# One decoder layer on one Trainium2 core: nine of 22 K-tile pairs of the down projection as seven block products

## The chip, the cores and the metric

The kernel runs on one core of a Trainium2 chip. The metric is device microseconds of that core, the median of several runs. The engines have queues of their own that run in order: TensorE (PE, with weight loads shown as PEld), VectorE (DVE), ScalarE (ACT), GpSimd (POOL) and SyncE (SP, which here only issues DMAs).

## The reference

One layer of a hybrid decoder, 256 tokens, model width 2048, all in float32. What matters here is its last third:

```python
x = x + jnp.concatenate([ha, hb], axis=-1) @ w_out[i]          # mixers' output

h = rms_norm(x, ffn_norm_g[i])
u = h @ w_up[i]                                                # 2048 -> 2 * 5632
a, g = jnp.split(u, 2, axis=-1)
a = causal_dwconv(a, conv_w[i], conv_b[i])
x = x + (jax.nn.gelu(a, approximate=False) * g) @ w_down[i]    # 5632 -> 2048

gate = jax.nn.sigmoid(rms_norm(x, ple_norm_g[i]) @ w_ple_gate[i])
x = x + gate * (p[i].astype(x.dtype) @ w_ple_proj[i])
```

Before it stand the RMS norm, the combined input projection, four mLSTM heads and eight attention heads.

## The kernel before

Every matrix product is made of float32r parts: an operand is cast by ACT to `hi`, and DVE subtracts to get `lo = raw - hi`. A product of two operands is then three matmuls, hi·hi, hi·lo and lo·hi, accumulated in one PSUM bank. The activations lie transposed, 128 features on the partitions, as tiles of 512 columns: 256 tokens of `hi`, then 256 of `lo` (`hT`, `catT`, `x2T`, `uT`, `x3T`). The weights stream in from HBM.

`run_stream` (L208) drives everything. A block is 1024 weight elements per partition. For each block it issues the load from the SP queue (L221) three blocks ahead into one of three `raw` buffers, splits it (L236 cast on ACT, L238 subtraction on DVE) three blocks ahead into one of four `hi`/`lo` buffers, and calls the block's function, which issues the matmuls. A scheduler then orders each engine's queue; what it made is shown below.

The stages in order are: the input projection and the mixers (a pool `mix` that is closed at the end), the output projection (`token_group`, L247, `resid`, L693), the up projection (`wide_group`, L300), the down projection (`token_group` with `uT`, L781 to L783) and the gate stage (L806 to L808).

- The up projection makes 512 features at a time, eight blocks for `a` and eight for `g`. `up_a` (L732) and `up_g` (L754) read the four banks out, do the convolution and GELU on ACT and DVE, and write two K tiles of `uT` at a time (L765).
- The down projection goes over four groups of 512 output columns. A group has 22 blocks; a block is two K tiles of 128 features by 512 columns, so the 22 blocks are the 22 pairs of K tiles. A block is 2 token halves x 2 K tiles x 3 matmuls (L266, L267, L268) of 512 columns. At the end of each group `resid` adds the two banks to `xs` (L696), transposes four K tiles of `x3T` (L698, L154, with the split at L145 and L146) and sums squares (L160).
- The gate stage goes over five groups of columns: first one block of the p projection (banks of tag `aux`), then the blocks of the gate (`mm`), whose end (`gate_done`, L791) makes the sigmoid, multiplies, adds `xs` and stores.

PSUM has two rings of four banks, `mm` and `aux`. The transposed rows of p (`pT`) are made beside the mixers (`load_conv`, L113).

Of the kernel before, what the change touches and what calls it, by code (L numbers as in the profile page):

```python
# [32 lines left out]
BLK = 1024  # L33
RAW, PARTS = 3, 4
AHEAD_DMA, AHEAD_SPLIT = 3, 3
PAD = 48

# [5 lines left out]
def layer_kernel(  # L43
# [11 lines left out]
    bp = ctx.enter_context(tc.tile_pool(name="big", bufs=1))  # L55
    wp = ctx.enter_context(tc.tile_pool(name="w", bufs=3))
    ps = ctx.enter_context(tc.tile_pool(name="ps", bufs=4, space=bass.MemoryType.PSUM))

# [3 lines left out]
    def f32(ap):  # L62
        return ap.bitcast(F32)
# [3 lines left out]

    g1 = cp.tile([16, P], F32, name="g1")
    act.dma_start(out=g1, in_=mix_norm_g[0].rearrange("(k c) -> k c", c=P))
# [18 lines left out]
    pool.memset(neghalf, -0.5)  # L88
    vrows = cp.tile([42, P], F32, name="vrows")
    for lo, n, src in (  # L90
# [19 lines left out]
    cT = cp.tile([P, 4 * KF], F32, name="cT")  # L110
    pT = bp.tile([P, 2, 512], F32R, name="pT")

    def load_conv(mp):  # L113
        def gen():
            cs = mp.tile([P, 512], F32, tag="qk", name="cs", bufs=2)
            act.dma_start(out=cs[0:88, 0:128], in_=conv_w[0, 0:2].rearrange("w (k c) -> (w k) c", c=P))
            act.dma_start(out=cs[0:44, 128:256], in_=conv_w[0, 2].rearrange("(k c) -> k c", c=P))
            act.dma_start(out=cs[44:88, 128:256], in_=conv_b[0].rearrange("(k c) -> k c", c=P))
            pr = mp.tile([P, 512], F32, tag="qk", name="pr", bufs=2)
            act.dma_start(out=pr.rearrange("p (t d) -> p t d", t=NT), in_=p[0, 0].rearrange("(t p) d -> p t d", p=P))  # L120
# [6 lines left out]
            yield  # L127
            bk = bank("aux", "pTp")
            for k in range(2):
                for t in range(NT):  # L130
                    pe.transpose(bk[:, k * 256 + t * P : k * 256 + (t + 1) * P],
                                 pr[:, t * 256 + k * P : t * 256 + (k + 1) * P], ident)
            for k in range(2):
                split_T(pT[:, k, :], bk[:, k * 256 : (k + 1) * 256])
            yield
        side.append(gen())
# [185 lines left out]

    apool = ctx.enter_context(tc.tile_pool(name="acts", bufs=1))
    aT = {}

    def new_aT(name):
        aT["cur"] = apool.tile([P, KD, 512], F32R, tag="aT", name=name)
        return aT["cur"]
# [3 lines left out]

    with tc.tile_pool(name="mix", bufs=1) as mp:
        catT = mp.tile([P, KD, 512], F32R, name="catT")

# [13 lines left out]

        hT = new_aT("hT")  # L350
        ssq1 = sm.tile([P, NT, 8], F32, name="ssq1")
        r1 = {}
# [367 lines left out]

    with tc.tile_pool(name="ffn", bufs=1) as fp:
        uT = fp.tile([P, KF, 512], F32R, name="uT")
# [3 lines left out]
        gl = {}  # L726

        def merge(dst, b):
# [3 lines left out]
        def up_a(q):  # L732
            st = {}

            def f(jj, b):
                pair, j = divmod(jj, 2)
                if j == 0:
                    st["a"] = fp.tile([P, 2, S], F32, tag="a", name="a", bufs=2)
                    st["c"] = gl[q, pair] = fp.tile([P, 2, S], F32, tag="gl", name="c", bufs=3)
# [12 lines left out]
            return f  # L752

        def up_g(q):  # L754
            st = {}

            def f(jj, b):
                pair, j = divmod(jj, 2)
                if j == 0:
                    st["u"] = fp.tile([P, 2, S], F32, tag="a", name="u", bufs=2)  # L760
                u, k = st["u"], 4 * q + 2 * pair
                merge(u[:, j], b)
                if j == 1:
                    dve.tensor_mul(u, u, gl.pop((q, pair)))
                    split_T(uT[:, k : k + 2, :], u)  # L765
            return f

        blocks = []
        x2 = aT["cur"]
        for q in range(KF // 4):  # L770
            blocks.extend(wide_group(w_up, q * 512, lambda: x2, up_a(q), "mm"))
            blocks.extend(wide_group(w_up, FF + q * 512, lambda: x2, up_g(q), "aux"))
        ssq3 = sm.tile([P, NT, 4], F32, name="ssq3")
# [17 lines left out]
        def gate_done(c0, n, last):  # L791
# [12 lines left out]
            return f  # L804

        for c0, n in ((0, 512), (512, 512), (1024, 512), (1536, 256), (1792, 256)):  # L806
            blocks.extend(token_group(w_ple_proj, [0], lambda: pT, c0, n, proj_done, tag="aux"))
            blocks.extend(token_group(w_ple_gate, all_k, get_x3T, c0, n, gate_done(c0, n, c0 == 1792)))  # L808
        run_stream(blocks, 0)

# [29 lines left out]
```

## Time and profile before

| | |
|---|---|
| median of 3 runs | 1286.85 us (1286.49 to 1286.88) |
| profiled execution, device time | 1286.34 us |
| its span | 1284.6 us |
| granted TensorE clock | 1.00 |
| moved by DMA | 238.69 MB, mean 186 GB/s |

The profile shows one execution. "Busy" of an engine is the time in which an instruction of it runs, and matmuls overlap each other, so a busy PE says only that it is not waiting. The table by stretches gives, for a window of the span, the busy time of each engine with the number of its instructions, the granted clock, the busy share of the DMA engines and GB/s. In the timeline, the bracket behind a row is the idle time of the engine ahead of it and what ended it.

### The profile page before, as it was taken

Reading aid. Unit: us, or ns where it says so; the run is one execution under the profiler, and the core shown is the slowest. Engines: PE = TensorE matmul, PEld = TensorE weight load, DVE = VectorE, ACT = ScalarE, POOL = GpSimd, SP = SyncE. Lnnn points to the kernel's source line nnn. Section 1 sums busy time; section 2 is a strip of 40 time slices with the busy share of each in tenths; the row PEclk is TensorE's granted clock in tenths of the full one; section 3 lists DMA queues with packets and bytes.
Section 4 is the critical chain, followed back from the end, with each engine's and each line's share of the span. In section 5 each row is a group of like instructions: output and inputs, shape, how many; then the busy total and the mean of one; then the engine's idle time right before and its main releaser. Section 6 shows DMA issues by size and latency. Waiting matters only on the chain.

```text
span 1284.6 us, 18150 instructions
## 1 busy us (share of the span) xinstructions
PE 1278.1 (99%) x7060; PEld 1123.1 (87%) x7060; DVE 754.3 (59%) x1008; ACT 650.7 (51%) x964; POOL 18.0 (1%) x33
## 2 busy tenths in 40 slices
PE   9999999999999999999999999999999999999998
PEld 7899999988888888888888888888888888888888
DVE  5455566554565565766676576767654545445554
ACT  7655454445554464655555455545543434444443
POOL 2000000000000000000000000000000000000000
PEclk9999999999999999999999999999999999999999
DMA  8676854556565666666666666666656566656663
GB/s 258 170 188 185 220 158 139 161 147 173 175 186 183 186 180 196 186 191 188 191 195 184 194 188 191 183 196 195 186 191 196 187 193 189 194 189 192 202 204 124
DMA packets 132040, 238.69 MB, mean 186 GB/s; under 512 B 7946, under 2 KB 28018, under 8 KB 131954
## 3 DMA queue, kind: packets, MB, share of 16 engines
q1 hardware_dynamic: 131072, 237.07, 62.8%
q8 instruction: 55, 0.90, 0.3%
q10 hardware_dynamic: 657, 0.43, 0.1%
q14 instruction: 32, 0.25, 0.1%
q0 software_dynamic: 224, 0.03, 0.0%
HBM read 235.40 MB, written 2.10 MB: 185 GB/s over the span
## 4 chain that ended last, share of the span: by engine, by line
PE 98%; DMA 1%; DVE 0%; ACT 0%; issue 0%; SPq 0%; DVEq 0%
PE wg L316 25%; PE tg L267 17%; PE tg L268 17%; PE tg L266 17%; PE wg L317 13%; PE fg L292 2%; PE fg L294 2%; PE fg L293 2%; DMA raw<-in_w_in_dram 1%; PE xT L154 1%; PE mob L609 0%; PE msc L583 0%; PE qkp L507 0%; PE sc L523 0%; PE ob L548 0%; PE rowb L494 0%
## 5 line engine op out<-in xcount | busy, mean ns | idle before, releaser
L238 DVE TENSOR_TENSOR lo<-raw,hi 128x1024 fp32r<-128x1024 f32 (+2 forms) x462 | 546.4, 1184 | 474.0 <-ACT hi L236 472.0
L236 ACT CAST hi<-raw 128x1024 fp32r<-128x1024 f32 (+2 forms) x462 | 470.6, 1019 | 557.3 <-PE tg L268 271.2
L316 PE MATMUL wg<-x2T,hi 128*128 128x512 f32 x1408 | 488.3, 392 | 0.0
L317 PE MATMUL wg<-x2T,lo 128*128 128x256 f32 x1408 | 393.5, 280 | 0.0
L316 PEld LDWEIGHTS wg<-x2T,hi 128*128 128x128 f32 x1408 | 264.1, 188 | 56.4
L317 PEld LDWEIGHTS wg<-x2T,lo 128*128 128x128 f32 x1408 | 267.3, 190 | 0.1
L266 PE MATMUL tg<-hi,uT 128*128 128x512 f32 x352 | 137.2, 390 | 0.0
L267 PE MATMUL tg<-lo,hT 128*128 128x512 f32 (+1 forms) x384 | 136.6, 356 | 0.5 <-DVE lo L238 0.5
L267 PE MATMUL tg<-lo,uT 128*128 128x512 f32 x352 | 137.0, 389 | 0.0
L268 PE MATMUL tg<-hi,uT 128*128 128x512 f32 x352 | 137.0, 389 | 0.0
L266 PE MATMUL tg<-hi,hT 128*128 128x512 f32 (+1 forms) x384 | 136.0, 358 | 0.0
L268 PE MATMUL tg<-hi,hT 128*128 128x512 f32 (+1 forms) x384 | 135.6, 354 | 0.0
L267 PEld LDWEIGHTS tg<-lo,hT 128*128 128x128 f32 x384 | 72.2, 188 | 8.1 <-DVE lo L238 0.9
L268 PEld LDWEIGHTS tg<-hi,hT 128*128 128x128 f32 x384 | 72.1, 188 | 7.4
L268 PEld LDWEIGHTS tg<-hi,uT 128*128 128x128 f32 x352 | 66.1, 188 | 13.7
L266 PEld LDWEIGHTS tg<-hi,uT 128*128 128x128 f32 x352 | 66.1, 188 | 13.7
L267 PEld LDWEIGHTS tg<-lo,uT 128*128 128x128 f32 x352 | 66.1, 188 | 13.6
L266 PEld LDWEIGHTS tg<-hi,hT 128*128 128x128 f32 x384 | 71.8, 188 | 6.9
L292 PE MATMUL fg<-hT,hi 128*128 128x256 f32 x256 | 74.3, 290 | 0.0
L294 PE MATMUL fg<-hT,lo 128*128 128x256 f32 x256 | 72.8, 284 | 0.0
L293 PE MATMUL fg<-hT,hi 128*128 128x256 f32 x256 | 72.4, 283 | 0.0
L267 PE MATMUL tg<-lo,x3T 128*128 128x512 f32 (+1 forms) x160 | 55.5, 347 | 0.0
(212 smaller groups left out, 1183.7 us busy)
## 6 DMA issues: line engine op xcount, KB each, us to landing
raw<-in_w_up_dram SPq DMA_DIRECT2D x176, 512.0 KB, 3.9
raw<-in_w_down_dram SPq DMA_DIRECT2D x88, 512.0 KB, 4.8
raw<-in_w_in_dram SPq DMA_DIRECT2D x79, 512.0 KB, 3.8
raw<-in_w_in_dram SPq DMA_DIRECT2D x48, 344.0 KB, 3.4
raw<-in_w_out_dram SPq DMA_DIRECT2D x32, 512.0 KB, 4.0
raw<-in_w_ple_gate_dram SPq DMA_DIRECT2D x32, 512.0 KB, 4.6
xs<-in_x_dram SPq DMA_DIRECT2D x8, 256.0 KB, 6.5
raw<-in_w_ple_proj_dram SPq DMA_DIRECT2D x3, 512.0 KB, 4.5
```

The costliest lines, as they stand in the source:

```text
L154: pe.transpose(bk[:, t * P : (t + 1) * P], xs[:, t, k * P : (k + 1) * P], ident)
L236: act.copy(hi, raw[:, :w])
L238: dve.tensor_sub(lo, raw[:, :w], f32(hi))
L266: pe.matmul(o, ah, hi[:, i, :], start=first, stop=False)
L267: pe.matmul(o, ah, lo[:, i, :], start=False, stop=False)
L268: pe.matmul(o, al, hi[:, i, :], start=False, stop=last)
L292: pe.matmul(o, hi[:, i, cols], a[:, 0:256], start=first, stop=False)
L293: pe.matmul(o, hi[:, i, cols], a[:, 256:512], start=False, stop=False)
L294: pe.matmul(o, lo[:, i, cols], a[:, 0:256], start=False, stop=last)
L316: pe.matmul(o, hi[:, i, cols], a, start=first, stop=False)
L317: pe.matmul(o[:, 256:512], lo[:, i, cols], a[:, 0:256], start=False, stop=last)
```

## The change

The down projection goes over two groups of 1024 columns instead of four of 512. In a group, a plain pair of K tiles is two units, each one K tile by 1024 columns, with eight block products in all (2 K tiles x 2 token halves x 2 column halves). Nine of the 22 pairs (2, 4, ... 18) take seven block products by the Strassen scheme in Winograd's form, in four units. The left operand's four sums (tokens x K) are made in the up stage by `left_sums`, split, written to HBM from POOL's queue, and read back once for each group from SP's. The right operand's four sums are made by DVE in place in the two raw buffers. Eight banks are open in a group: four output blocks, of which (1, 1) is fed by plain pairs alone, and four for the products P1, P5, P6, P7. After the ninth such pair `sums_done` adds the four to `xs`; after the last pair `add_rest` adds the others.

For this the raw buffers grow from three to five and the split buffers from four to seven in that part (they use the two temporaries of the up stage and the space of `x2T`), the activations get two buffers in one pool (`uT` becomes `uA` and `uB`), p is loaded and transposed at the start of the down projection, and the p projection of each gate group stands in the middle of its gate blocks. `run_units` takes the place of `run_stream` from the up projection on.

```diff
+RAW2, PARTS2 = 2, 3
+SEVEN = (2, 4, 6, 8, 10, 12, 14, 16, 18)
...
+        def left_sums(p_, u):
+            (a11, a21), (a12, a22) = ((u[:, j, 0:P], u[:, j, P:S]) for j in range(2))
+            f = sm.tile([P, 512], F32, tag="junk", name="Sf").rearrange("p (i c) -> p i c", i=4)
+            dve.tensor_add(f[:, 0], a21, a22)
+            dve.tensor_sub(f[:, 1], f[:, 0], a11)
+            dve.tensor_sub(f[:, 2], a11, a21)
+            dve.tensor_sub(f[:, 3], a12, f[:, 1])
+            t = fp.tile([P, 4, 256], F32R, tag="pT", name="Sp")
+            act.copy(t[:, :, 0:P], f)
+            dve.tensor_sub(t[:, :, P:256], f, f32(t[:, :, 0:P]))
+            pool.dma_start(out=sums[SEVEN.index(p_)], in_=f32(t).rearrange("p i c -> p (i c)"))
...
+        def run_units(us, first_late):
...
+                while True:
+                    if loaded < len(us) and held + len(us[loaded].srcs) <= RAW + RAW2 * more:
+                        us[loaded].load(loaded)
...
+                    elif split < min(loaded, i + PARTS + PARTS2 * more):
+                        us[split].split(split)
...
+                u.fn(*u.parts)
...
+            def product(key, ah, al, hi, lo):
...
+                pe.matmul(o, ah, hi, start=first, stop=False)
+                pe.matmul(o, ah, lo, start=False, stop=False)
+                pe.matmul(o, al, hi, start=False, stop=last)
...
+                def split1(hi, lo):
+                    v = late["S"][:, SEVEN.index(p_) % 2]
+                    nc.sync.dma_start(out=f32(v).rearrange("p i c -> p (i c)"), in_=sums[SEVEN.index(p_)])
+                    st["S"] = v
+                    part(hi[:, 0:512], lo[:, 0:512], first.raws[0][:, 0:512])
+                def fn1(hi, lo):
+                    product("P1", *left(k, 0), half(hi, 0), half(lo, 0))
+                def split2(hi, lo):
+                    part(hi, lo, first.raws[1])
+                def fn2(hi, lo):
+                    product((0, 0), *left(k + 1, 0), half(hi, 0), half(lo, 0))
+                    product((0, 1), *S(4), half(hi, 1), half(lo, 1))
+                def split3(hi, lo):
+                    ra, rb_ = first.raws
+                    dve.tensor_sub(half(ra, 0), half(ra, 1), half(ra, 0))
+                    dve.tensor_sub(half(ra, 1), half(rb_, 1), half(ra, 1))
+                    part(hi, lo, ra)
+                def fn3(hi, lo):
+                    product("P5", *S(1), half(hi, 0), half(lo, 0))
+                    product("P7", *S(3), half(hi, 1), half(lo, 1))
+                def split4(hi, lo):
+                    ra, rb_ = first.raws
+                    dve.tensor_sub(half(rb_, 1), half(rb_, 1), half(ra, 0))
+                    dve.tensor_sub(half(rb_, 0), half(rb_, 0), half(rb_, 1))
+                    part(hi, lo, rb_)
+                def fn4(hi, lo):
+                    product((1, 0), *left(k + 1, 1), half(hi, 0), half(lo, 0))
+                    product("P6", *S(2), half(hi, 1), half(lo, 1))
...
-        for c in range(4):
-            blocks.extend(token_group(w_down, list(range(0, KF, 2)), lambda: uT, c * 512, 512,
-                                      resid(c, ssq3, get_x3T, g_ple)))
...
+        us += down(0, "mm", "aux", sums_done(0), add_rest(0), {0: make_pT})
+        us += down(1024, "aux", "mm", sums_done(1024), add_rest(1024),
+                   {40: transposes(0), 41: transposes(2), 42: transposes(4, 6)})
```

Here `part(hi, lo, raw)` is the cast and the subtraction of before, the second and third arguments of `down` are the rings of the output banks and of the P banks, and `transposes(k)` makes two K tiles of `x3T`.

How the queues stand, at three places. Names carry running numbers; `hi248` is the `hi` part of unit 248, and `w2` is the space of `x2T`, which holds three of the seven split buffers and the left sums. On PE, one block of the down projection before, two K tiles by 512 columns:

```order
L266 MATMUL tg0_10185<-hi261_10471,uT_4383 128x512
L267 MATMUL tg0_10185<-lo261_10472,uT_4383 128x512
L268 MATMUL tg0_10185<-hi261_10471,uT_4383 128x512
L266 MATMUL tg0_10185<-hi261_10471,uT_4383 128x512
L267 MATMUL tg0_10185<-lo261_10472,uT_4383 128x512
L268 MATMUL tg0_10185<-hi261_10471,uT_4383 128x512
```

On PE after the change, the first four of the seven products of pair 4 in the second group (`dn(t, n)` are the output banks):

```order
L882 MATMUL dnP1_9950<-hi248_9945,uA_4373 128x512
L883 MATMUL dnP1_9950<-lo248_9946,uA_4373 128x512
L884 MATMUL dnP1_9950<-hi248_9945,uA_4373 128x512
L882 MATMUL dn(0, 0)_9875<-w2_8987,uA_4373 128x512
L883 MATMUL dn(0, 0)_9875<-w2_8987,uA_4373 128x512
L884 MATMUL dn(0, 0)_9875<-w2_8987,uA_4373 128x512
L882 MATMUL dn(0, 1)_9879<-w2_8987 128x512
L883 MATMUL dn(0, 1)_9879<-w2_8987 128x512
L884 MATMUL dn(0, 1)_9879<-w2_8987 128x512
L882 MATMUL dnP5_9970<-w2_8987 128x512
L883 MATMUL dnP5_9970<-w2_8987 128x512
L884 MATMUL dnP5_9970<-w2_8987 128x512
```

A product keeps its three matmuls of 512 columns; P7, (1, 0) and P6 follow. On DVE, inside the down projection before, nothing stands between the `lo` subtractions:

```order
L238 TENSOR_TENSOR lo236_9994<-raw236_9991,hi236_9993 128x1024
L238 TENSOR_TENSOR lo237_10012<-raw237_10009,hi237_10011 128x1024
L238 TENSOR_TENSOR lo238_10030<-raw238_10027,hi238_10029 128x1024
L238 TENSOR_TENSOR lo239_10048<-raw239_10045,hi239_10047 128x1024
L238 TENSOR_TENSOR lo240_10066<-raw240_10063,hi240_10065 128x1024
```

On DVE after, pair 6 of the first group (units 192 to 195) with the plain pair behind it (units 196, 197):

```order
L837 TENSOR_TENSOR lo192_9170<-raw192_0_9108,hi192_9169 128x512
L837 TENSOR_TENSOR w2_8987<-raw192_1_9110,w2_8987 128x1024
L930 TENSOR_TENSOR raw192_0_9108<-raw192_0_9108 128x512
L931 TENSOR_TENSOR raw192_0_9108<-raw192_1_9110,raw192_0_9108 128x512
L940 TENSOR_TENSOR raw192_1_9110<-raw192_1_9110,raw192_0_9108 128x512
L837 TENSOR_TENSOR lo196_9212<-raw196_0_9126,hi196_9211 128x1024
L941 TENSOR_TENSOR raw192_1_9110<-raw192_1_9110 128x512
L837 TENSOR_TENSOR w2_8987<-raw192_0_9108,w2_8987 128x1024
L837 TENSOR_TENSOR lo197_9230<-raw197_0_9139,hi197_9229 128x1024
L837 TENSOR_TENSOR w2_8987<-raw192_1_9110,w2_8987 128x1024
```

Where four `lo` subtractions stood for two pairs, there are six, of them one half as wide, and four half-wide subtractions in place. SP's queue issues the loads for the next pair of seven products in this order (the sum comes from `sums`):

```order
L822 DMA raw198_0_9189<-in_w_down_dram 128x1024
L913 DMA w2_8987<-sums_4390 128x1024
L822 DMA raw202_0_9203<-in_w_down_dram 128x1024
L822 DMA raw198_1_9191<-in_w_down_dram 128x1024
L822 DMA raw203_0_9215<-in_w_down_dram 128x1024
```

The two halves of a pair are now two loads, with others between. The third place is the start of the gate stage. On PE before, the gate's first matmuls follow the last of the down projection:

```order
L267 MATMUL tg1_10186<-lo263_10508,uT_4383 128x512
L268 MATMUL tg1_10186<-hi263_10507,uT_4383 128x512
L266 MATMUL tg0_10629<-hi265_10543,x3T_9306 128x512
L266 MATMUL tg1_10630<-hi265_10543,x3T_9306 128x512
L267 MATMUL tg0_10629<-lo265_10544,x3T_9306 128x512
```

On PE after:

```order
L884 MATMUL dn(1, 1)_9887<-w2_8987,uB_4374 128x512
L149 MATMUL xT0_10667<-ident_94,xs_81 128x128 x2
L149 MATMUL xT1_10672<-ident_94,xs_81 128x128 x2
L149 MATMUL xT2_10695<-ident_94,xs_81 128x128 x2
L261 MATMUL tg0_10775<-w2_8987,x3T_10666 128x512
L262 MATMUL tg0_10775<-w2_8987,x3T_10666 128x512
```

On ACT after, at the same place:

```order
L836 CAST w2_8987<-raw305_0_10616 128x1024
L155 ACTIVATE junk_10761,ssq3_4391<-xs_81 128x512
L836 CAST w2_8987<-raw306_0_10634 128x1024
L140 ACTIVATE x3T_10666<-xT0_10667,vT_113 128x256
L140 ACTIVATE x3T_10666<-xT1_10672,vT_113 128x256
```

The sixteen K tiles of `x3T` now all stand behind the last matmul of the down projection, and the first of their casts stands behind the cast of unit 306.

More of the change, by code (lines that the diff above doesn't have):

```diff
@@ L88, in layer_kernel @@
     pool.memset(neghalf, -0.5)
-    vrows = cp.tile([42, P], F32, name="vrows")
+    vrows = mp.tile([42, P], F32, name="vrows")
     for lo, n, src in (
@@ L126, in gen @@
             dve.tensor_copy(cT, bk[:, :176])
[L127 to L134, printed above, removed]
             yield
@@ L350, in layer_kernel @@
         hT = new_aT("hT")
+        catT = new_aT("catT")
         ssq1 = sm.tile([P, NT, 8], F32, name="ssq1")
@@ L726, in layer_kernel, with temp @@
         gl = {}
+        sums = kp.tile([len(SEVEN), P, 1024], F32, name="sums")
+        def temp(name):
+            return fp.tile([P, BLK], F32, tag="tmp", name=name, bufs=RAW2)
         def merge(dst, b):
@@ L764, in f @@
                     dve.tensor_mul(u, u, gl.pop((q, pair)))
-                    split_T(uT[:, k : k + 2, :], u)
-            return f
[L768 to L772, printed above, removed]
+                    dst = uA[:, k : k + 2, :] if k < KD else uB[:, k - KD : k - KD + 2, :]
+                    split_T(dst, u)
@@ new lines, in layer_kernel, with __init__, load, split @@
+        class Unit:
+            def __init__(self, srcs, fn, split=None, frees=1, shift=0):
+                self.srcs, self.fn, self.own, self.frees, self.shift = srcs, fn, split, frees, shift
+            def load(self, j):
+                self.raws = []
+                for i, src in enumerate(self.srcs):
+                    kb, n = src.shape[1], src.shape[2]
+                    raw = new_raw(f"raw{j}_{i}")
+                    nc.sync.dma_start(out=raw[:, : kb * n].rearrange("p (k n) -> p k n", k=kb), in_=src)
+                    self.raws.append(raw)
+            def split(self, j):
+                hi, lo = new_parts(j, self.shift)
+                if self.own is not None:
+                    self.own(hi, lo)
+                    self.parts = hi, lo
+                    return
+                kb, n = self.srcs[0].shape[1:3]
+                part(hi[:, : kb * n], lo[:, : kb * n], self.raws[0][:, : kb * n])
+                self.parts = [v[:, : kb * n].rearrange("p (k n) -> p k n", k=kb) for v in (hi, lo)]
@@ new lines, in part, with units @@
+        def part(hi, lo, raw):
+            act.copy(hi, raw)
+            dve.tensor_sub(lo, raw, f32(hi))
+        def units(blocks):
+            return [Unit([b[0]], b[1], shift=b[4] if len(b) > 4 else 0) for b in blocks]
+        def run_units(us, first_late):
+            loaded = split = held = 0
+            for i, u in enumerate(us):
+                if i == first_late:
+                    w2 = new_aT("w2").rearrange("p k n -> p (k n)")
+                    v = w2[:, 0 : 6 * BLK].rearrange("p (u n) -> p u n", n=BLK)
+                    late.update(hi=v[:, 0:3], lo=v[:, 3:6], S=w2[:, 6 * BLK :].rearrange("p (b i c) -> p b i c", b=2, c=256))
+                more = i >= first_late
+                while True:
+                    if loaded < len(us) and held + len(us[loaded].srcs) <= RAW + RAW2 * more:
+                        us[loaded].load(loaded)
+                        held += len(us[loaded].srcs)
+                        loaded += 1
+                    elif split < min(loaded, i + PARTS + PARTS2 * more):
+                        us[split].split(split)
+                        held -= us[split].frees
+                        split += 1
+                    else:
+                        break
+                u.fn(*u.parts)
```

154 lines of the change are left out of this document (138 added, 16 removed).

## The prediction

> **What bounds the kernel now.** I read the page's busy table and chain first, then the table by stretches, then the timeline of single instructions.
>
> ```profile
> PE 1278.1 (99%) x7060; PEld 1123.1 (87%) x7060; DVE 754.3 (59%) x1008; ACT 650.7 (51%) x964; POOL 18.0 (1%) x33
> PE 98%; DMA 1%; DVE 0%; ACT 0%; issue 0%; SPq 0%; DVEq 0%
> ```
>
> PE is busy for 1278.1 of 1284.6 us, and the chain that ended last runs on PE for 98% of the span. The time is the number of matmuls times their spacing, plus 6.5 us at both ends.
>
> ```profile
> 460.00:937.70 477.70, 477.70 (x2759) 422.43 (x2758) 322.78 (x453) 257.23 (x346) 0.00 (x0) 1.00 0.66 190
> 937.70:1180.00 242.30, 242.30 (x1083) 200.88 (x1082) 120.13 (x115) 102.65 (x116) 0.00 (x0) 1.00 0.61 191
> 1180.00:1280.00 100.00, 100.00 (x547) 87.30 (x546) 52.73 (x60) 43.94 (x52) 0.69 (x1) 1.00 0.58 183
> ```
>
> The three stretches are the up projection, the down projection and the gate stage (columns: length, then busy PE, PEld, DVE, ACT, POOL, granted clock, DMA share, GB/s). PE has no gap in any of them and its granted clock is 1.00. In the down stretch DVE is busy 120.13 of 242.30 us, ACT 102.65, DMA engines 0.61 at 191 GB/s: that is the room which the change draws on.
>
> The instructions that read `uT` (count, least/median/greatest ns, first and last start), and three matmuls of the timeline (start, length):
>
> ```profile
> L266 PE MATMUL tg<-hi,uT x352: 389/389/476, 937.9 to 1179.3; 128*128 128x512 f32 x176
> ```
>
> ```profile
> 957.68 0.39 PE L266 MATMUL tg<-hi,uT 128*128 128x512 f32 x1
> 957.91 0.39 PE L267 MATMUL tg<-lo,uT 128*128 128x512 f32 x1
> 958.13 0.39 PE L268 MATMUL tg<-hi,uT 128*128 128x512 f32 x1
> 958.36 0.39 PE L266 MATMUL tg<-hi,uT 128*128 128x512 f32 x1
> ```
>
> One matmul's 0.39 us overlaps the next. What counts is the spacing: 958.36 − 957.68 = 0.68 us for three, **0.2267 us** each. 352 x 3 = 1056 of them give 239.4 of the 242.3 us; the rest is transposes.
>
> **The change, part by part.** *Matmuls removed.* A seven-product pair issues 21 instead of 24 matmuls for 1024 columns, of the same 128x512 shape. Nine pairs in two column groups: 9 x 2 x 3 = 54 fewer, and the order of the new program has 1002 where 1056 stood. With PE never waiting, 54 x 0.2267 = **−12.24 us**.
>
> The Trainium skill, "TensorE: Matmul & The Clock Gate", section "Back-to-back issue gap", gives an isolated warm matmul N/2.4 + 2.5 ns, 215.8 ns for 512 columns; by that the term would be an estimated 11.65 us. The row's spacing is 226.7 ns, so the row decides.
>
> *Work added to VectorE and ScalarE.* Two pieces of the timeline, of DVE and of ACT:
>
> ```profile
> 938.46 0.68 DVE L764 TENSOR_TENSOR u<-u,c 128x512 f32<-128x512 f32 x1
> 939.10 1.23 DVE L238 TENSOR_TENSOR lo<-raw,hi 128x1024 fp32r<-128x1024 f32 x1
> 940.24 0.42 DVE L730 TENSOR_TENSOR u<-wg,u 128x256 f32<-128x256 f32 x1
> 940.58 0.68 DVE L143 TENSOR_TENSOR uT<-u,uT 128x512 fp32r<-128x512 f32 x1
> 941.18 0.68 DVE L764 TENSOR_TENSOR u<-u,c 128x512 f32<-128x512 f32 x1
> ```
>
> ```profile
> 913.05 1.05 ACT L236 CAST hi<-raw 128x1024 fp32r<-128x1024 f32 x1 [1.72 <-PE wg L316]
> 914.01 0.37 ACT L729 COPY a<-wg 128x256 f32<-128x256 f32 x1
> ```
>
> Back to back, a 1024-wide two-input op holds DVE for 940.24 − 939.10 = 1.14 us and a 512-wide one for 941.18 − 940.58 = 0.60 us; a cast holds ACT for 0.96 us. The in-place subtraction of half a weight tile has no row of its own; L764 reads two SBUF tiles of that size, so I take 0.60 us (0.68 if nothing overlaps). A seven-product pair needs four of these, one 512-wide and three 1024-wide `lo`: 5 x 0.60 + 3 x 1.14 = 6.42 us (7.12 with no overlap). A plain pair needs 2 x 1.14 = 2.28 us. They alternate, so a period of both is 8.70 us of DVE (9.57 by durations) against 45 x 0.2267 = **10.20 us of PE**. ACT has 0.56 + 5 x 0.96 = 5.4 us. PE keeps the longer total; the queue order decides whether it waits. The printed orders hide each cast behind another subtraction (`lo196` and `lo197` stand between the dependent ones), so I charge no steady loss, 0 to +9 us.
>
> *Weight buffers.* A seven-product pair holds two of the five raw buffers until its third and fourth splits. The page's DMA issues (count, KB, median us to landing), the landings of all raw loads, and the first 30 us by engine:
>
> ```profile
> raw<-in_w_down_dram SPq DMA_DIRECT2D x88, 512.0 KB, 4.8
> ```
>
> ```profile
> DMA to landing us min/median/max: 2.8/4.0/6.9
> ```
>
> ```profile
> 0.00:30.00 30.00, 27.74 (x136) 23.13 (x137) 17.99 (x28) 23.00 (x55) 7.17 (x23) 1.00 0.87 261
> ```
>
> In the looser order shown (pair of `raw192`) the first half is free 6.42 us after the pair begins on DVE. The next pair's second half is loaded into that buffer (the queue has `raw198_1` last), lands 4.8 us later and is wanted 1.2 us into that pair: a loop of 6.42 + 4.8 − 1.2 = 10.0 us, 0.2 us under PE's 10.2. In the tighter order it is 8.9. From a landing of about 5.0 us the looser loop is the longer. The demand is five 0.524 MB loads (four weights, one stored sum) in 10.2 us, 257 GB/s; the first 30 us moved 261 GB/s at a share of 0.87, so it fits. Working the first three seven-product pairs through by these durations, DVE waits about 1.9 us for each second half and is level with PE at `hi195`/`lo195`; afterwards it pulls ahead. I charge **+0.7 us**, ends 0 and +6.
>
> The Trainium skill, "DMA: Bandwidth & Descriptors", section "Anatomy of one DMA", fits 2.0 us plus bytes/436 GB/s for POOL-issued transfers, an estimated 3.2 us here; by it the loop would be 8.4 us and this term zero. The median landing in the trace is 4.8 us, so I keep the row.
>
> *Left sums.* Nine times in the up stage: four 128-wide subtractions, a 512-wide cast and `lo`, one 512 KB write from POOL's queue.
>
> ```profile
> 34.20 0.28 DVE L167 TENSOR_SCALAR dg<-ident,rstd_mix 128x128 f32<-128x128 f32 x1
> ```
>
> No two-input 128-wide row exists; 0.28 us has one input, 0.42 us twice the width; I take 0.28. 9 x (4 x 0.28 + 0.68) = 16 us raise DVE from 322.8 to 339 of 477.7 us. Four units of split weights (2.7 us of PE each) cover a burst of 1.8 us: cost 0; without cover at most 16 us. POOL has 0.00 us of work in that stretch, and the first sum is read back long after it is written.
>
> *Moved work.* The input-p transposes and casts move from the mixer to the first down unit: the same instructions, 0. The group sums and residual additions are about 5.2 + 2.4 us of DVE per half, beside three and two plain pairs: 0. The end of the second half is different. Its four result banks are the `aux` ring that the x3T transposes need, so now **all** of them stand behind the last matmul; before, 12 of 16 were done.
>
> ```profile
> 1179.77 0.39 PE L268 MATMUL tg<-hi,uT 128*128 128x512 f32 x1
> ...
> 1180.20 1.06 ACT L236 CAST hi<-raw 128x1024 fp32r<-128x1024 f32 x1 [1.67 <-PE tg L268]
> ...
> 1184.77 1.03 PE L154 MATMUL xT<-ident,xs 128*128 128x128 f32 x8
> 1185.40 1.57 ACT L145 ACTIVATE x3T<-xT,vT 128x256 fp32r<-128x256 f32 x4 [1.43 <-PE xT L154]
> 1185.56 0.48 PE L266 MATMUL tg<-hi,x3T 128*128 128x512 f32 x1
> 1185.91 1.66 DVE L146 SCALAR_TENSOR_TENSOR x3T<-xT,vT,x3T 128x256 fp32r<-128x256 f32 x4 [0.68 <-ACT x3T L145]
> ```
>
> On ACT the cast of `raw306` stands ahead of the first x3T cast, and its target is freed by the last down matmul: it starts 0.2 us after that matmul's slot (1180.20 against 1179.77 + 0.23) and holds ACT 0.96 us. The x3T cast takes about 0.48 more, so the first gate matmul comes near 1.7 us. PE has 0.3 us of transposes meanwhile (eight take 0.8 us): 1.4 us idle. The fifth transpose pair then waits about 0.45 us for a bank, which DVE reads only after `lo306`. Sum **+1.8 us**; queued behind that cast are all x3T casts, for which PE waits. Ends: 0 (the cast lands early) and +4.
>
> Sum: −12.24 + 0.7 + 1.8 = −9.7. The profiled execution is 1286.34 us, its span of 1284.6 plus 1.74 around it, giving 1276.6. The median of the runs lies 0.5 above it: **1277.1 us**.
>
> **The rivals.**
>
> *DVE is the bound in the seven-product periods.* In-order waits push its 9.57 us of durations past 10.2, say to 10.7. For: PE is in order too, and a late `lo` holds every product behind it. Against: room of 0.6 to 1.5 us. 18 x 0.5 = 9 us, less some 2 us of stock built up on plain pairs at the ends of each half: 1284.
>
> *The weight loop is the bound; slower.* Place: the SP queue's load of a second half. Taking the middle of the two loops, 9.45 at a landing of 4.8, PE waits from 5.55 us on, 18 x (landing − 5.55). From a median landing of 6.3 us (18 x 0.72 = 13) the kernel is slower than before; at 6.9, the trace's largest, 18 x 1.35 = 24 us give 1300. Against: at 261 GB/s the early weight loads still landed, and rows of 4 KB replace rows of 2 KB.
>
> *The gain never reaches PE's end.* A mixture of smaller waits of these two, 1284 to 1289. That fewer matmuls are not issued at all is excluded by the order.
>
> **How the numbers follow.** Forecast (1274 to 1281): 0.75. DVE bound, 1281 to 1284.3: 0.11. Between, within 0.2% of 1286.85: 0.06. Weight loop, above 1289.4: 0.08. A measurement of this kernel can tell about 0.2% (2.6 us) from no change. Faster 0.86, same 0.06, slower 0.08. Low end 1273.8: the matmul term alone gives 1274.6 on the runs' median. High end 1284: the DVE case is inside, the other two (0.14) are left out.
>
> **What would show it.** Right: PE MATMUL rows of the two halves sum to 1002 at 0.2267 us, PE idle in them near 0 to 1 us, one gap of 1 to 2 us where x3T begins. DVE bound: PE idle before `lo` products with DVE at 9 tenths. Loop bound: ACT casts waiting on `raw<-in_w_down_dram`, landings above 5.5 us. Wrong in sign: PE idle over 12 us in all.

## The result and the profile after

| | before | after |
|---|---|---|
| median | 1286.85 us (7 runs, 1286.49 to 1288.41) | 1279.86 us (7 runs, 1276.99 to 1283.47) |
| profiled execution, device time | 1286.34 us | 1280.42 us |
| its span | 1284.6 us | 1278.7 us |

The ratio is 0.9944 with a 95% interval of 0.9931 to 0.9957: faster by 7.0 us, where 9.7 was forecast. The page of the changed kernel, the engines' busy times and the chain that ended last:

```profile
PE 1269.0 (99%) x7006; PEld 1112.0 (87%) x7006; DVE 851.3 (67%) x1173; ACT 681.8 (53%) x1011; POOL 23.6 (2%) x43
PE 92%; DMA 3%; DVE 3%; ACT 1%; issue 0%; SPq 0%; DVEq 0%; ACTq 0%
```

PE is still the bound, but 6% of the chain has moved from PE to DMA, DVE and ACT: somewhere PE now waits for weights. (The share says through which engines the chain runs; it is not the time that is lost.) The table by stretches of the changed kernel (columns as before) says where; the rows are the up projection, the two halves of the down projection, and the entry of the gate stage:

```profile
460.00:937.70 477.70, 477.70 (x2758) 422.42 (x2757) 334.73 (x497) 261.59 (x354) 5.60 (x10) 1.00 0.68 201
938.50:1055.00 116.50, 114.97 (x505) 93.60 (x504) 101.76 (x115) 62.60 (x70) 0.00 (x0) 1.00 0.76 257
1055.00:1168.80 113.80, 113.80 (x503) 94.25 (x502) 101.24 (x111) 64.62 (x74) 0.00 (x0) 1.00 0.75 250
1168.80:1175.00 6.20, 5.53 (x28) 3.82 (x27) 5.56 (x13) 5.24 (x14) 0.72 (x1) 1.00 0.61 194
```

The left sums in the up projection cost PE nothing, though DVE rose from 322.78 to 334.73 us. The second half of the down projection has no idle PE either. The first half has, and so has the gate's entry. Who waited for whom, the three longest of PE's rows from 937 us on:

```profile
PE dn(1, 0)_9017 L882 <- ACT hi L836: 0.8, 1, 0.8
PE xT L149 <- DVE xs L995: 0.4, 2, 0.3
PE dn(0, 0)_9009 L883 <- DVE lo L837: 0.4, 1, 0.4
```

These count idle PE only; a matmul that starts into an empty pipeline costs more than its wait. So I count starts. From the first matmul of the down projection to the last one of the gate stage the kernel before took 342.19 us (937.93 to 1280.12). Without 54 matmuls of 0.2267 us, and with the four p transposes that now stand there (about 0.4 us), 330.4 would remain. The changed kernel took 335.2 (938.53 to 1273.69), so **4.8 us were lost there**: 1.9 at the gate's entry and 2.9 within the down projection. The latter runs from 938.53 to 1168.80, 230.27 us; 1001 spacings of 0.2267 and the p transposes make 227.3.

The larger of two places of loss on PE, in the timeline:

```profile
1015.56 0.39 PE L884 MATMUL dnP<-hi,w 128*128 128x512 f32 x1
1016.74 0.50 PE L882 MATMUL dn(1, 0)_9017<-hi,uB 128*128 128x512 f32 x1 [0.79 <-ACT hi L836]
1017.08 0.39 PE L882 MATMUL dnP<-hi,w 128*128 128x512 f32 x1
1017.69 0.50 PE L882 MATMUL dn(0, 0)_9009<-hi,uB 128*128 128x512 f32 x1 [0.22 <-ACT hi L836]
```

The starts 1015.56 to 1016.74 and 1017.08 to 1017.69 lie 1.18 and 0.61 us apart instead of 0.23: 1.33 us. What was late is found on DVE, seven microseconds earlier:

```profile
1008.27 0.69 DVE L930 TENSOR_TENSOR raw<-raw 128x512 f32<-128x512 f32 x1
1010.77 0.69 DVE L931 TENSOR_TENSOR raw<-raw,raw 128x512 f32<-128x512 f32 x1 [1.81 <-DMA raw<-in_w_down_dram]
```

L931 is the first DVE instruction of the pair that reads its second raw half. The loads on SP just before:

```profile
1004.25 0.33 SPq L822 DMA_DIRECT2D raw<-in_w_down_dram  x1
1005.39 0.33 SPq L822 DMA_DIRECT2D raw<-in_w_down_dram  x1
```

The program's order names them: after `raw216_0` stand the reload of the sum, then `raw221_0`, then `raw216_1`. `raw216_0` and `raw216_1` are the two K tiles of a seven-product pair. The second was loaded behind a plain weight that is wanted three units later. It landed 5.3 us after its issue, and ACT and DVE stood still until then. The other place is the same: `raw202_0` (971.54) stands ahead of `raw198_1` (973.27), and

```profile
979.61 0.69 DVE L931 TENSOR_TENSOR raw<-raw,raw 128x512 f32<-128x512 f32 x1 [2.77 <-DMA raw<-in_w_down_dram]
981.98 0.50 PE L883 MATMUL dn(0, 0)_9009<-lo,uB 128*128 128x512 f32 x1 [0.39 <-DVE lo L837]
```

The two places make 1.33 and 0.83 us; the rest of the 2.9 lies in gaps of less than 0.2.

A load of the down projection also lands later than before: by the page's DMA issues in that stretch 5.5 us (median), where it was 4.8.

```profile
raw<-in_w_down_dram SPq DMA_DIRECT2D x83, 512.0 KB, 5.5
w<-sums SPq DMA_DIRECT2D x18, 512.0 KB, 5.1
```

Outside this stretch the profiled executions differ by 1.1 us against the changed kernel: its first 38 us were 0.84 us longer (PE reaches `rstdb` at 38.04 instead of 37.20), of which 0.2 came back where the p transposes left the mixer, and 0.5 more lies behind the last matmul (5.0 instead of 4.5 us to the end of the span). In the first 37 us all engines have the same instructions in the same order, and between the traces of the runs below both times differ by as much (37.8 to 40.1 and 4.6 to 5.3 us). But all of these lie above the one trace of before, so whether a part of it comes with the change stays open.

### The profile page after: what moved, and what is told of

It is laid out like the page before. It is cut to its first block, busy times and chain, and to the rows that moved or that the text cites. A ratio compares the mean times of both kernels' runs of the same rounds, so it can differ in the third digit from the quotient of the medians.

```text
span 1278.7 us, 18356 instructions
## 1 busy us (share of the span) xinstructions
PE 1269.0 (99%) x7006; PEld 1112.0 (87%) x7006; DVE 851.3 (67%) x1173; ACT 681.8 (53%) x1011; POOL 23.6 (2%) x43
## 4 chain that ended last, share of the span: by engine, by line
PE 92%; DMA 3%; DVE 3%; ACT 1%; issue 0%; SPq 0%; DVEq 0%; ACTq 0%
PE wg L311 25%; PE wg L312 13%; PE tg L263 11%; PE tg L262 10%; PE tg L261 10%; DMA raw<-in_w_down_dram 2%; PE fg L287 2%; PE fg L289 2%; PE fg L288 2%; DMA raw<-in_w_in_dram 1%; DVE w L837 1%; PE dnP L884 1%; PE dnP L883 1%; PE dnP L882 1%; PE dn(0, 0)_9875 L884 1%; PE dn(0, 0)_9875 L882 1%
## 5 line engine op out<-in xcount | busy, mean ns | idle before, releaser
L837 DVE TENSOR_TENSOR lo<-raw,hi 128x1024 fp32r<-128x1024 f32 (+1 forms) x268 | 320.3, 1203 | 177.2 <-ACT hi L836 176.3
L836 ACT CAST hi<-raw 128x1024 fp32r<-128x1024 f32 (+1 forms) x268 | 275.5, 1035 | 280.1 <-PE wg L311 177.4
L233 DVE TENSOR_TENSOR lo<-raw,hi 128x1024 fp32r<-128x1024 f32 (+2 forms) x161 | 179.5, 1116 | 159.5 <-ACT hi L231 158.9
L231 ACT CAST hi<-raw 128x1024 fp32r<-128x1024 f32 (+2 forms) x161 | 154.6, 960 | 174.0 <-PE tg L263 100.4
L836 ACT CAST w<-raw 128x1024 fp32r<-128x1024 f32 x69 | 67.4, 988 | 57.9 <-DMA raw<-in_w_down_dram 22.1
L837 DVE TENSOR_TENSOR w<-raw,w 128x1024 fp32r<-128x1024 f32 x69 | 78.2, 1143 | 24.8 <-ACT w L836 24.4
L261 PE MATMUL tg<-hi,catT 128*128 128x512 f32 x128 | 50.3, 393 | 0.0
L263 PE MATMUL tg<-hi,catT 128*128 128x512 f32 x128 | 50.0, 390 | 0.0
L262 PE MATMUL tg<-lo,catT 128*128 128x512 f32 x128 | 49.8, 389 | 0.0
```

The source lines that it names most:

```text
L231: act.copy(hi, raw[:, :w])
L233: dve.tensor_sub(lo, raw[:, :w], f32(hi))
L261: pe.matmul(o, ah, hi[:, i, :], start=first, stop=False)
L262: pe.matmul(o, ah, lo[:, i, :], start=False, stop=False)
L263: pe.matmul(o, al, hi[:, i, :], start=False, stop=last)
L836: act.copy(hi, raw)
```

## The experiments

All runs, with the ratio to the kernel before on the same chip. "Lost" is the time from the first down matmul to the last gate matmul over what the matmuls need, worked out as above from one trace (342.19 − 0.2267 x matmuls removed + 0.4).

| run | median us (range, runs) | ratio, 95% | lost us |
|---|---|---|---|
| after | 1279.86 (1276.99 to 1283.47, 7) | 0.9944, 0.9931 to 0.9957 | 4.8 |
| a1_again | 1279.63 (1278.25 to 1280.12, 5) | 0.9935, 0.9921 to 0.9948 | 4.5 |
| e1_no_pairs | 1289.39 (1288.56 to 1291.46, 11) | 1.0018, 1.0010 to 1.0027 | 2.0 |
| e2_x3t_banks | 1278.15 (1276.13 to 1279.69, 5) | 0.9930, 0.9916 to 0.9943 | 1.9 |
| e3_reload_pool | 1277.19 (1276.98 to 1277.90, 5) | 0.9924, 0.9912 to 0.9937 | 2.8 |
| e4_no_reload | 1280.21 (1279.12 to 1280.66, 5) | 0.9944, 0.9931 to 0.9956 | 3.0 |
| e5_six_pairs | 1282.43 (1281.74 to 1283.33, 5) | 0.9960, 0.9948 to 0.9973 | 2.5 |
| e6_both | 1276.17 (1275.95 to 1277.99, 4) | 0.9915, 0.9901 to 0.9929 | 0.9 |
| e7_one_less | 1279.45 (1277.67 to 1280.91, 4) | 0.9937, 0.9923 to 0.9950 | 2.2 |
| e8_from_3 | 1283.30 (1282.67 to 1284.33, 5) | 0.9968, 0.9956 to 0.9980 | 7.0 |
| e9_four | 1320.42 (1316.81 to 1321.58, 4) | 1.0250, 1.0237 to 1.0263 | 44 |
| e10_both_from_3 | 1283.51 (1281.73 to 1283.81, 5) | 0.9964, 0.9951 to 0.9976 | 8.2 |
| e11_ten_pairs | 1289.40 (1286.86 to 1295.36, 12) | 1.0016, 1.0006 to 1.0025 | 12.8 |

Runs a1, e5, e6, e7 share a chip and the runs of before, as do e1 to e4, and e8 to e11.

### The frame without the pairs

```diff
-SEVEN = (2, 4, 6, 8, 10, 12, 14, 16, 18)
+SEVEN = ()
...
-        sums = kp.tile([len(SEVEN), P, 1024], F32, name="sums")
```

> No pair is multiplied in seven products: all 22 pairs take the eight, in the new frame (groups of 1024 columns, one weight load per K tile, x3T behind the last down matmul). 54 matmuls of 0.2267 us come back: +12.24 us. Theory L (the loss of 2.5 us inside the down projection belongs to the seven-product pairs: buffers, landings, DVE) with the gate entry as measured (2.6 us): 1279.9 + 12.24 - 2.5 = 1289.6, and a spread between runs as narrow as before's (under 1 us). Rival, the whole loss sits in the pairs and the gate entry costs nothing of its own: 1286.9. Rival, the frame itself is slow (loads of 4 KB rows, the order of the banks): above 1291, PE idle in the down stretch although there are no pairs.

Measured 1289.39, theory L's time to 0.2 us and 2.4 above before. The down projection took 239.65 us from first to last matmul, where 1055 spacings and the p transposes make 239.6: no loss. The gate's entry cost the same as with pairs (1.95 us from the last down matmul to the first gate matmul, 0.23 before). The eleven runs lie 2.9 us apart, wider than theory L's 1. So the loss within the down projection belongs to the pairs, and the entry to the new frame.

### The gate's entry

```diff
-    def transpose_x(dst, k0, g):
+    def transpose_x(dst, k0, g, tag="aux"):
-            bk = bank("aux", f"xT{k}")
+            bk = bank(tag, f"xT{k}")
-        return lambda *_: [transpose_x(get_x3T(), k0, g_ple) for k0 in ks]
+        return lambda *_: [transpose_x(get_x3T(), k0, g_ple, "mm" if k0 < 8 else "aux") for k0 in ks]
```

> The x3T transposes of K tiles 0 to 7 take banks of the ring that the sums of the pairs have given back, so they can stand among the last down matmuls again; nothing else is changed. Theory G (the gate entry costs about 2.6 us because all transposes stand behind the last down matmul): first gate matmul within 0.5 us of the last down matmul instead of 1.95 us, time 1277 to 1278.5. Rival: two transposes of later K tiles now stand ahead of the first gate matmul and wait for the residual additions of the second half, which are made on DVE after the last down matmul: 1 to 2 us of idle PE stay, time 1279 to 1280.

Some 12 of 32 transposes went back among the last down matmuls, and the stretch lost 1.9 instead of 4.8 us. Up to the last pairs, loads and splits stand in this program as in the changed kernel. Taken apart, 1.5 us were lost in the down projection and 0.4 from there on, where it was 1.9 in the changed kernel and without pairs. So the transposes behind the last matmul are what the entry cost, as theory G had it. The median fell by 1.7, within the forecast, though its range overlaps that of the changed kernel. The first gate matmul comes 1.48 us after the last down one, not within 0.5: the transposes of later K tiles stand ahead of it, as the rival said.

### The reload of the sums

```diff
-                    nc.sync.dma_start(out=f32(v)..., in_=sums[SEVEN.index(p_)])
+                    pool.dma_start(out=f32(v)..., in_=sums[SEVEN.index(p_)])
```

> The stored left sums are read back by POOL's queue instead of SP's. In the changed kernel SP waited 30.2 us (11 times, longest 4.6) for PE before such a read, with weight loads queued behind it. Theory Q (this wait holds weight loads up): the waits of ACT for weight loads (44.6 us) fall below half, the 2.5 us of PE idle in the down projection go, time 1277.4, spread between runs under 2 us. Rival B (the buffers, not the queue, decide when a load starts): waits and time stay, 1279.9 within 1 us, spread stays at some 5 us.

The time is theory Q's to 0.2 us, and five runs lie within 0.9 us. (The intervals of the two ratios overlap, so a gain of some 2 us is likely rather than certain.) But the mechanism isn't shown to be Q's. ACT's waits for weight loads fell from 44.6 to 35.1 us, not below half, and two more traces of the changed kernel's program (a1 and e7 below) have 36.3 and 34.4:

```profile
ACT w L836 <- DMA raw<-in_w_down_dram: 19.3, 16, 3.3
ACT hi L836 <- DMA raw<-in_w_down_dram: 15.8, 12, 2.5
```

And in the changed kernel's own trace a reload never directly held up a weight load: the next load was issued 1.8 to 7.0 us after it, when a buffer came free. What differs is the order. In this program `raw216_1` stands ahead of `raw221_0`, and at the place where DVE had waited 1.81 us it goes straight on:

```profile
1009.53 0.69 DVE L930 TENSOR_TENSOR raw<-raw 128x512 f32<-128x512 f32 x1
1010.25 0.69 DVE L931 TENSOR_TENSOR raw<-raw,raw 128x512 f32<-128x512 f32 x1
```

The 1.33 us of PE near 1016 are gone. `raw202_0` still stands ahead of `raw198_1`; there DVE waited 2.13 us, and PE lost 0.29 instead of 0.83. The run e7 below shows that a trace can lack the stall near 1016 with the old order too, so the trace alone does not prove that the order did it.

```diff
+                    if SEVEN.index(p_) < 2:
                         nc.sync.dma_start(out=f32(v)..., in_=sums[SEVEN.index(p_)])
```

> Only the first two stored sums are read back in each half, the later pairs use these again: the output is not the reference's. It takes the wait out of SP's queue as the run before does, and also 0.52 MB of every 10.2 us of traffic, 257 to 205 GB/s. Theory T (traffic stretches the landings, which feed the buffer loop): median landing of a weight load from 5.4 back to about 4.8 us, time 1277.4, while the run with POOL's queue stays at 1279.9. Theory Q: as that run, 1277.4 in both. If VectorE's work decides, neither changes: 1279.9.

The median landing went from 5.5 to only 5.3 us, with 230 and 216 GB/s in the two halves instead of 257 and 250, so the mean traffic isn't what stretches it: theory T falls. The median stayed at 1280.2, where theory Q wanted 1277.4, although 14 of the 18 reloads are gone from SP's queue; that speaks against theory Q. The order of the loads fits both runs: here `raw221_0` (1002.57) still stands ahead of `raw216_1` (1004.31), and PE still stalled there, by 0.38 us. The trace lost 1.8 us less than the changed kernel's, but it is that of the fastest of the five (1279.12), and traces of one and the same program differ by more than that, as e7 shows. It also began the down projection 0.3 us later and ended 0.3 later behind its last matmul.

### Again, and with fewer pairs

The changed kernel unaltered:

> The changed kernel once more, on the chip of the next three, since its seven runs lay 6.5 us apart (1276.99 to 1283.47) and those of the kernel before 1.9. Theory J (the buffer loop of the pairs has so little room that the landings of single loads decide, so the spread is the kernel's own): median 1279.9 within 1 us, spread 3 us or more. Rival, the spread came with the chips of the earlier runs: under 1.5 us here. In the second trace theory J expects PE's stalls in the down projection at the same pairs but of other lengths than 1.05 and 1.33 us.

The median agrees, the spread is 1.9 us, between the two theories. The stalls stand at the same two places, 1.05 and 0.86 us long instead of 0.83 and 1.33: the order fixes the places, the landings the lengths.

```diff
-SEVEN = (2, 4, 6, 8, 10, 12, 14, 16, 18)
+SEVEN = (2, 5, 8, 11, 14, 17)
```

> Six pairs (every third) in seven products instead of nine (every second), nothing else: 18 matmuls come back, +4.1 us, and a pair has 15.6 us of PE time instead of 10.2 for the same loop of buffers. Theory L (the loop of buffers and landings costs the 2.2 us of stalls): no stall over 0.3 us in the down projection, 1279.9 - 2.2 + 4.1 = 1281.8, spread under 2 us. Rival, the stalls do not come from the density of the pairs: 1284.0 and a spread as wide as with nine.

1282.43, 2.8 above nine pairs on the same chip, where 18 matmuls alone make 4.1: the three pairs more bring back only two thirds of their matmuls. One stall was left, of 0.44 us at 953. Theory L's 1281.8 was 0.6 low.

### Both edits together

> The two edits of before together: x3T through the freed banks, sums read back by POOL's queue. If they are independent: 1277.2 - 1.7 = 1275.5, spread under 2 us. If the gain of the POOL queue came from another order of VectorE's splits (three pairs stand otherwise there than in the changed kernel) that this program does not share: near 1278, stalls again near the sixth or seventh pair.

1276.17, 0.7 above the sum of both gains, and all four runs lie below all five of a1 on that chip (of the four of e7 below, the same program as a1, one lies at 1277.67). `raw216_1` stands ahead of `raw221_0` here too. PE's waits from 937 us on are down to one:

```profile
PE xT L149 <- DVE xs L995: 0.3, 1, 0.3
```

This is the best version found: 11.3 us under before on that chip, of 12.24 us of matmuls.

### Buffers

```diff
-                    if loaded < len(us) and held + len(us[loaded].srcs) <= RAW + RAW2 * more:
+                    if loaded < len(us) and held + len(us[loaded].srcs) <= RAW + (RAW2 - 1) * more:
```

> Four raw weight buffers are filled in the down projection instead of five; nothing else. Theory L: each buffer is then used once in a period of 10.2 us, held for at least 6.4 us by the first half of a pair and 7.5 by the second, and filled in 5.4 us, so a period takes 11.8 to 12.9 us: 18 x 1.6 to 2.7 = 29 to 49 us, time 1309 to 1329. If VectorE's work decides, the buffers have room and the time stays within 3 us of 1279.9.

1279.45, by the expectation the end of theory L. But the edit does not do what I took it for. It changes where loads are written in the program, and the scheduler puts them back: with running numbers left out of the names, every queue holds the same instructions in the same order with the same waits as in the changed kernel, and the loads go to the same five buffers. In the trace `raw221_0` (1002.24) still stands ahead of `raw216_1` (1003.37). So the run tests neither the buffers nor the order. It is the changed kernel a third time, and the medians of the three runs agree: 1279.86, 1279.63, 1279.45.

Its trace is the more telling. The down projection took 227.71 us and lost 0.4, where the other two traces of this program lost 2.9 and 2.7; at the two places PE now lost less than 0.2. The three traces part at one load: `raw180_1`, the second half of the first pair, landed 4.6 us after its issue at 938.62, where it took 6.6 and 6.7 in the other two, and the weight loads from `raw185_0` on were issued 1.5 to 3 us sooner (`raw216_1` at 1003.37 instead of 1005.39). One and the same program thus loses 0.4 to 2.9 us there in one execution. A single trace of another run that differs by less than that (e3, e4 or e5) does not show what its edit did.

```diff
-                if made[0] % (RAW + RAW2) in range(1, RAW2 + 1):
-                    return temp(name)
+                if made[0] % (RAW + 1) == 1:
+                    return late["raw"]
...
-                    late.update(hi=v[:, 0:3], ...
+                    late.update(raw=temp("rawt"), hi=v[:, 0:3], ...
...
-                    if loaded < len(us) and held + len(us[loaded].srcs) <= RAW + RAW2 * more:
+                    if loaded < len(us) and held + len(us[loaded].srcs) <= RAW + 1 * more:
```

> Four raw weight buffers in the down projection and the gate, now in fact: one temporary tile is used over and over instead of two in turn. The run with one less in flight had changed the order of the loads and not the number of buffers. Theory L as in that run: a buffer is used once in a period of 10.2 us, held 6.4 us or more by a pair and filled in 5.4: period 11.8 to 12.9 us, 29 to 49 us slower, 1309 to 1329. Rival (buffers have room, lead and order of the loads decide the stalls): within 5 us of 1279.7.

1320.42, 40.8 above nine pairs with five buffers and within theory L's 29 to 49. In the trace the down projection is 30.8 us longer than the changed kernel's, and the gate's entry, with two waits of PE of 3.7 and 3.5 us for the residual additions, 7.2 us. The waits of this kernel from 937 us on:

```profile
ACT hi L836 <- DMA raw<-in_w_down_dram: 44.6, 19, 5.3
ACT w L836 <- DMA raw<-in_w_down_dram: 34.9, 21, 3.0
DVE raw L931 <- DMA raw<-in_w_down_dram: 23.3, 10, 3.8
```

So with four buffers the loop of buffers and landings is what the pairs hang on; VectorE's rate isn't, its work was the same. That five are only just enough is inferred from this and from ACT's waits for loads with five (44.6 us); no run had six.

### The pairs elsewhere

```diff
-SEVEN = (2, 4, 6, 8, 10, 12, 14, 16, 18)
+SEVEN = (3, 5, 7, 9, 11, 13, 15, 17, 19)
```

> The nine pairs are 3, 5, ... 19 instead of 2, 4, ... 18: three plain pairs stand ahead of the first one in each half, and two behind the last. Theory S (in the first half the splits begin with a lead of only some 3 us over PE, in the second with 11; the stalls come where the first half uses this lead up): a longer lead, no stall over 0.3 us in the first half, 1279.7 - 2.2 = 1277.5, and up to 1 us back where the sums of the second half now have two plain pairs beside them. Rival (the rate of the pairs is what is short, not the lead): stalls of 1 us near the fifth to seventh pair as before, 1279.7.

Slower by 3.6 us than the 1279.7 expected. The changed kernel itself was not run on this chip; by the ratios (0.9968 against 0.9935 to 0.9944) it is 3 to 4 us. So theory S is wrong as I put it. One more plain pair gave no lead: PE's first product of the first pair came at 956.1 and DVE's first subtraction in it at 953.1, 3 us ahead, as before. The order shows why: `raw186_0` and `raw187_0` are loaded ahead of `raw182_0` and `raw182_1`, the two halves of the first pair, and take two of the five buffers; the first half, issued at 944.5, landed at 951.7, and ACT waited 2.74 us for it. Three stalls of 1.0 to 1.2 us followed in the first half. The gate's entry took 2.52 instead of 1.95 us, with a wait of 1.0 for the residual additions.

> x3T through the freed banks, sums read back by POOL's queue, and the pairs 3 to 19. That program without the later pairs had one small stall or none, so theory S gains nothing more in the down projection: 1276.2 within 0.7 us. If the sums with two plain pairs beside them hold up the x3T transposes, which now need the sums' banks: 1277 to 1278, with PE idle behind the last pair.

Wrong too: the entry is what costs here. Two plain pairs don't cover the sums, the residual additions and the x3T splits on DVE, which was busy without a gap from 1160 to 1176 us. PE waited, and then its clock fell (below).

> x3T through the freed banks, sums read back by POOL's queue, and ten pairs (2, 4, ... 16, 17, 19): six more matmuls leave, -1.36 us. Pairs 16 and 17 stand side by side: 12.8 us of VectorE beside 9.5 us of PE, 3.3 us out of the lead. Theory S: the second half has that lead (11 us) and loses nothing, the first half has 3 to 4 us by then and may lose up to 2: 1274.8 to 1276.2. Rival, the two pairs hold four of five buffers and the loads between them come late: over 1277, PE idle near 1037 and 1155 us.

1289.40, 13 us above nine pairs with both edits, instead of 1.4 below. The edit does two things: it adds a tenth pair, and it puts the last pair at 19. The run before has the latter with nine pairs and lies 7 us above them, so the 13 us are not the tenth pair's alone. Near 1038 to 1043 PE lost 1.7 us. Most was lost at the gate's entry, where again two plain pairs stand behind the last seven-product pair:

```profile
1168.54 0.39 PE L884 MATMUL dn(1, 1)_9906<-hi,uB 128*128 128x512 f32 x1
1169.68 0.44 PE L149 MATMUL xT<-ident,xs 128*128 128x128 f32 x2 [0.75 <-DVE x3T L141]
1172.95 0.69 PE L149 MATMUL xT<-ident,xs 128*128 128x128 f32 x2 [2.83 <-DVE x3T L141]
```

## Why the prediction was right, and where it was off

- **Matmuls removed, −12.24: right.** The two halves have 1002 matmuls at 0.2267 us, and with both edits 11.3 of the 12.24 us arrive. The page of the Trainium skill ("TensorE: Matmul & The Clock Gate", section "Back-to-back issue gap") would have given an estimated 11.65 us by its formula for an isolated warm matmul, 215.8 ns; this trace's spacing, of 0.2267 us, holds.
- **VectorE's work, 0: right.** In the first half DVE is busy 101.76 of 116.50 us; with the same work and one buffer less the time rose by 40.8, and with the same work in the same order the loss was 0.4 us in one trace and 2.9 in another. Its subtractions last 0.69 and 1.22 us, about as taken. (From the rows shown, the sums with no overlap are 7.09 and 9.55 us, not 7.12 and 9.57; nothing hangs on it.)
- **Weight buffers, +0.7: the step that was mis-sized; it was 2.9 in the profiled execution, and 2.7 and 0.4 in two more of this program.** The loop was the right one, and I gave its turning point as a landing of about 5.0 us. But I put the landing at the median of before, 4.8, where the changed kernel has 5.5, and took the queue's order to cost one wait of 1.9 us for each second half which the stock would cover. At 5.5 the looser loop is 6.42 + 5.5 − 1.2 = 10.7 us, over PE's 10.2. If every pair went by it, 18 x 0.5 = 9 us would be lost, so it holds at a few places only. The plain weights that are loaded ahead of a pair's second half (`raw202_0` ahead of `raw198_1`, which stood in the order I had printed, and `raw221_0` ahead of `raw216_1`) are where it struck in two of the three traces.
- **Left sums, 0: right.** PE had 477.70 of 477.70 us.
- **Gate entry, +1.8: right in size, 1.9 measured, and in the wait that ended last.** The first gate matmul starts 1.95 us after the last down one (1170.75 against 1168.80), where about 1.7 was forecast. The chain on ACT is the one given:

```profile
1169.28 1.05 ACT L836 CAST w<-raw 128x1024 fp32r<-128x1024 f32 x1 [0.64 <-ACT junk L155]
1170.23 0.83 ACT L140 ACTIVATE x3T<-xT,vT 128x256 fp32r<-128x256 f32 x2
1170.75 0.19 PEld L261 LDWEIGHTS tg<-w,x3T 128*128 128x128 f32 x1 [0.28 <-ACT x3T L140]
```

The cast of `raw306` starts 0.25 us after the last down matmul's slot, the x3T cast behind it, and the first gate matmul's weights wait for that. What the prediction did not have is a second chain beside it: the second and third pair of transposes wait for the residual additions (L995), and by them alone the gate would have begun only 0.2 us sooner. The fifth pair of transposes then waited for a bank, as forecast (L141, 0.21 us of idle PE).

- **p transposes, 0: right** within 0.2: 0.4 us in the down projection, 0.2 less in the mixer.
- **The sum.** In the profiled executions: −12.24 + 2.9 + 1.9 + 0.2 and 1.3 of start and end (0.84 + 0.5) give −5.9, and −5.9 were measured. The medians differ by 7.0, and by 7.9 and 8.0 where the same program ran again (a1 and e7). Against −9.7 the buffers' term is 2.2 in the profiled execution; how much of the 1.3 is the change's stays open.
- **The rivals.** DVE as the bound did not come. The weight loop as the bound, slower than before, came only where it was made so, with four buffers (1320). But of the signs named for it, ACT casts that wait for raw loads and landings above 5.5 us, the first was there and the second just reached; and PE was idle for 1.5 us in the two halves, not 0 to 1. The kernel stood nearer to that than the chance of 0.08 says: one buffer from it.

What stays open: why the changed kernel's runs spread (6.5 us over the first seven, 1.9 and 3.2 over the next five and four, 0.9 in e3). Three traces of its program differ by 2.6 us in what was lost, all of it in the down projection, and there by when single loads landed; what makes a load land late is not shown. That the order and not the queue made e3 faster fits e3, e4 and e6, but in e3 and e6 the splits and products of units 210 to 224 stand partly in another order too, and no run changed the order of the two loads alone.

## What to carry to other kernels

When a change makes each buffer be held longer, work out the loop hold + landing + order against the period with the landing that the new traffic will have, and look in the printed queue for loads that stand ahead of one wanted sooner: that is worth more than the mean share of the DMA engines. A ring of buffers that is just enough makes single executions of one program differ by microseconds. So take several traces of the unaltered program before you read a difference between two traces as the effect of an edit, and look whether the edit changed the queues at all. An accumulation that keeps more banks open pushes whatever used those banks behind its end; plan its exit, the sums and the next stage's operands, as carefully as its inner loop.

## What the runs showed of the chip

**A wait can cost more than its length, through the clock.** With four buffers PE waited twice in 1.5 us near 1129, 1.15 and 0.77 us:

```profile
1128.76 0.49 PE L882 MATMUL dn(0, 0)_9860<-hi,uB 128*128 128x512 f32 x1 [1.15 <-ACT hi L836]
1130.02 0.50 PE L883 MATMUL dn(0, 0)_9860<-lo,uB 128*128 128x512 f32 x1 [0.77 <-DVE lo L837]
1130.36 0.48 PE L884 MATMUL dn(0, 0)_9860<-hi,uB 128*128 128x512 f32 x1
1130.63 0.63 PE L882 MATMUL dn(0, 1)_9864<-hi,w 128*128 128x512 f32 x1
1131.06 0.63 PE L883 MATMUL dn(0, 1)_9864<-lo,w 128*128 128x512 f32 x1
```

From 1130.63 on the same matmuls start 0.43 us apart, eight of them, before the spacing is 0.23 again: half speed for 3.4 us, 1.6 us more on top of the waits. In the run with ten pairs the granted clock (the column behind POOL) stood at 0.50 for 8 us after the gate's entry:

```profile
1168.00:1172.00 4.00, 1.37 (x7) 0.63 (x5) 4.00 (x6) 3.20 (x6) 0.00 (x0) 0.95 0.85 268
1172.00:1176.00 4.00, 1.78 (x5) 0.92 (x6) 4.00 (x8) 1.62 (x5) 0.00 (x0) 0.50 0.69 229
1176.00:1180.00 4.00, 3.42 (x13) 2.57 (x13) 4.00 (x9) 3.54 (x11) 0.00 (x0) 0.50 0.51 168
```

The stalls of the changed kernel, 0.8 us at most, left its clock at 1.00. With four buffers one wait of 2.77 us (before 999.20) was followed by half speed, but one of 2.00 (before 982.06) and two of 1.58 and 1.21 within 5 us (before 1024.39 and 1029.19) left it at 1.00, so the length of the waits alone does not decide. The Trainium skill, "TensorE: Matmul & The Clock Gate", section "What's actually happening", has the half clock come after at least one idle window of about 3.4 us. No wait near 1129 was that long: two of 1.15 and 0.77 us were enough, so by these runs it is not one unbroken idle window that counts.

**Landings follow the spacing of the loads more than the mean traffic.** In the changed kernel the load issued at 971.54, 5.4 us after the DMA before it, landed in 3.8 us; the one of 1005.39, 1.1 us behind another, in 5.3. Of all loads of the down projection whose landing the trace has, the 10 issued more than 3 us after the one before took 3.9 us (median), the 29 issued less than 1.4 us behind one 5.8. With 10 to 14% less traffic (e4) the median was 0.2 us shorter.
